# A streaming-encoder block on one core: head transfers, gate merge, last product and row-factor broadcast moved

## The chip, the core and the metric

The kernel runs on one core of a Trainium2 chip. The metric is device microseconds of one execution. The core has TensorE (PE, matmuls; PEld is its weight load), VectorE (DVE), ScalarE (ACT), GpSimd (POOL) and SyncE (SP, which issues most transfers); each works through a queue of its own, in order, and they wait for one another by semaphores.

## The reference, cut to what matters

One layer on x of 256 tokens by 2048 channels, all in float32. Two token mixers (16-head stick-breaking attention and a Mamba-2 state-space scan, "SSD") work on the same normalised input; their outputs are merged by sigmoid gates, projected, normalised and added to x. A gated MLP with a short convolution follows, is normalised and added too.

```python
h = rms_norm(x, norm_mix_pre)                    # row factor * x * gain
proj = h @ w_in
q, k, v, z, xbc, dt, g_sb, g_ssd = split(proj)
o_sb = stick_breaking_attention(q, k, v)
xbc = silu(causal_dwconv(xbc, ssd_conv_w, ssd_conv_b))
dt = softplus(dt + dt_bias)
y = rms_norm((ssd_scan(xs, dt, a, bm, cm) + xs * d_skip) * silu(z), ssd_norm)
merged = sigmoid(g_sb) * (o_sb @ w_sb_proj) + sigmoid(g_ssd) * (y @ w_ssd_proj)
x = x + rms_norm(merged @ w_out, norm_mix_post)
u = causal_dwconv(rms_norm(x, norm_ffn_pre) @ w_up, ffn_conv_w, ffn_conv_b)
gate, val = split(u)
x = x + rms_norm((gelu(gate) * val) @ w_down, norm_ffn_post)
```

## The kernel before

**Weights as a stream.** All weights lie in one array of units of 128 x 1024 floats (512 KB), in the order of use. SP loads each unit into one of five raw buffers (`load`). `prep` splits it: ACT rounds it to a high half (`whi`, L67), DVE subtracts to get the low half (`wlo`, L68); five buffers of each. `unit` hands unit u to the matmuls after it has traced the splits up to u + 3. Activations are split in the same way, and a product is high x high, high x low and low x high, added up in PSUM: two passes with a 512-column and one with a 256-column operand for the "feature" products (`feat_run`, L123 and L125), three 512-column passes for the "token" products (`tok_step`, L152 to L154).

**The order of work.** A compile-time scheduler writes each engine's queue. Among instructions that it reckons ready it takes the one traced first; inside `tc.high_priority()` instructions count as traced at the program's start; inside `tc.manual_schedule(engines=...)` the named engines keep the traced order; `tc.issue_after(ins)` queues what the block traces on `ins`'s engine behind `ins`. From the second SSD group to the end of that stage PE keeps the traced order (L495, closed at L539); before that, and from L541 on, the scheduler orders PE, except in the two hand-written stretches (L726 to L869, and the end from L936).

**The head (L206 to L246).** Twelve wake matmuls on a tile of ones (two passes each) run while the first data come. ACT's queue issues a transfer of the gain `gpre`; SP's queue issues x's first chunk (four k-tiles of x transposed, 512 KB), unit 0 in two halves, unit 1, and then three more chunks of x between units 2 to 4, the vectors and the rest. A hand-written order for ACT and DVE then makes, for each chunk, the high half (ACT, x times gain, L239) and the low half (DVE, L240) of the four k-tiles, with a split of unit 0's first half after two of them and of the second half after four; unit 0's splits are ACT, DVE, ACT, DVE. The first matmuls (`ps_first`, units 0 to 7, `feat_mms`) use them. All products are made with x times gain alone; the row factor of the norm comes in later.

**The row factor of x.** x is loaded once more by rows (`xt`, L249). ACT squares and sums the rows (L482), `rsqrt_mean` makes the factor on DVE and ACT (L280 to L285), all at high priority. `tok_to_bc` (L287) then spreads it: DVE makes two diagonals (`rx_dg`, L293, high priority), PE multiplies ones by them (`rx_ps`, L294), DVE copies the result (`rstd_bc`, L295). It is called after the products `ps_xs` of units 8 and 9 (L503), and once more for the MLP's factor (L898). `dt_work` multiplies by `rstd_bc` (L315), makes softplus in a chain of small DVE and ACT steps, and PE transposes the two results (`dt_pt`, L334 and L335) at a fixed place among the `ps_z` products.

**The merge (L641 to L649).** For each quarter n of the channels, `ps_sb` is finished, DVE multiplies it into the gate (L645) and adds the other mixer's part (L646), for two row tiles; PE then transposes the merged rows (`ptm`, L469) at places among the next products. After n = 3 these are the products `ps_mo`.

**The end (L919 to L955).** The last product `ps_fo` is finished for the first row tile ahead of the second (`tok_mm_lag`). For each row tile, in hand-written order: ACT squares and sums the last 512 columns (`n3.add`, L665), ACT and DVE make a first estimate of the row factor (`n3.last`, L686 to L688), DVE multiplies the PSUM result by the gain (`gained`, L917), DVE refines the factor (`n3.newton`, L692 and L693), and then the rows are scaled, added to x and stored.

Of the kernel before, what the change touches and what calls it, by code (L numbers as in the profile page):

```python
# [10 lines left out]
F32 = mybir.dt.float32  # L11
F32R = mybir.dt.float32r
AF = mybir.ActivationFunctionType
ALU = mybir.AluOpType
# [3 lines left out]
P = 128  # L18
T = 256
KT = 16  # L20
# [7 lines left out]
C_FW = C_CB + 48  # L28
C_FB = C_FW + 88 * 3
C_D = C_FB + 88  # L30
C_N = KT + C_D + 64

LNEXP = "natural_log_exp_and_others"
PE = {mybir.EngineType.PE}
# [5 lines left out]


@with_exitstack
def block_kernel(ctx, tc, xT, xN, wts, vecs, rows, hvec, gain, out):


    nc = tc.nc
    n_units = wts.shape[0]

    const = ctx.enter_context(tc.tile_pool(name="const", bufs=1))
    wraw = ctx.enter_context(tc.tile_pool(name="wraw", bufs=RBUFS))  # L50
    wspl = ctx.enter_context(tc.tile_pool(name="wspl", bufs=WBUFS))
# [7 lines left out]
    def slot(dtype, shape, name):  # L59
        return slots.tile([P] + shape, dtype, tag="slot", name=name)  # L60

    def act_chunk(name):

        return slot(F32R, [4, 2, T], name)

    def split(hi, lo, src):
        nc.scalar.copy(hi, src)  # L67
        nc.vector.tensor_tensor(lo, src, hi.bitcast(F32), op=ALU.subtract)  # L68

    def lnexp():  # L70

        tc.keep_in_program_order(nc.scalar.preload_act_table_set(LNEXP))


    raw_t, spl_t = {}, {}
    state = {"u": 0, "at": 0}

    def load(u, parts=1):
        raw = wraw.tile([P, 1024], F32, tag="raw", name=f"raw{u}")
        n = 1024 // parts  # L80
        for i in range(parts):
            state["load"] = nc.sync.dma_start(raw[:, i * n:(i + 1) * n], wts[u][:, i * n:(i + 1) * n])
        raw_t[u] = raw

    def prep(parts=1):

        v = state["u"]
        state["u"] += 1
        if v not in raw_t:
            load(v)  # L90
        raw = raw_t.pop(v)
        hi = wspl.tile([P, 1024], F32R, tag="whi", name=f"whi{v}")
        lo = wspl.tile([P, 1024], F32R, tag="wlo", name=f"wlo{v}")
        spl_t[v] = (hi, lo)
        n = 1024 // parts
        for i in range(parts):
            w = slice(i * n, (i + 1) * n)
            split(hi[:, w], lo[:, w], raw[:, w])
            yield

    def unit(ahead=WBUFS - 2):
# [31 lines left out]
    def feat_mm(acts, name, ahead=WBUFS - 2):  # L133
        ps = mm_bank(name)
        for u in range(2):
            feat_run(w_tiles(range(8 * u, 8 * u + 8), [ps], ahead), acts, u == 0)
        return ps
# [18 lines left out]
    def tok_mm(acts, nk, name, beats=(3, 7, 11, 15)):  # L156

        pss = [mm_bank(f"{name}_{t}") for t in range(2)]
        for k in range(nk):
            if k % 2 == 0:  # L160
                hi, lo = unit()
            for t in range(2):
                tok_step(pss, acts, k, nk, t, hi, lo)
            for _ in range(beats.count(k % 16)):
                pump()
        return pss
# [34 lines left out]
    def drain():  # L201
        while bg:
            pump()


    ones = const.tile([P, P], F32, name="ones")  # L206
    nc.vector.memset(ones, 1.0)
    wake = paux.tile([P, 512], F32, tag="aux", name="wake")
    for i in range(12):
        nc.tensor.matmul(wake[:, :P], ones, ones, start=True, stop=True)  # L210
    gpre = const.tile([P, KT], F32, name="gpre")
    nc.scalar.dma_start(gpre, vecs[:, 0:KT])
    vec = const.tile([P, C_N - KT], F32, name="vec")
    a_ch, x_raw = [], []
    for c in range(4):
        x_raw.append(slot(F32, [4, T], f"x{c}"))
    raw0 = wraw.tile([P, 1024], F32, tag="raw", name="raw0")
    raw_t[0] = raw0
    nc.sync.dma_start(x_raw[0], xT[:, 0:4, :])
    for i in range(2):  # L220
        nc.sync.dma_start(raw0[:, i * 512:i * 512 + 512], wts[0][:, i * 512:i * 512 + 512])
    load(1)
    for c in range(1, 4):
        nc.sync.dma_start(x_raw[c], xT[:, 4 * c:4 * c + 4, :])
        for u in range(2 * c, min(2 * c + 2, RBUFS)):
            load(u)

    nc.sync.dma_start(vec, vecs[:, KT:])
    hv = const.tile([P, 2], F32, name="hv")
    nc.sync.dma_start(hv, hvec)  # L230
    na = const.tile([P, 1], F32, name="na")
    with tc.manual_schedule(engines=ACT_DVE):
        lnexp()
        for c in range(4):
            ac = act_chunk(f"a{c}")
            steps = prep(2 if c == 0 else 1)
            for j in range(4):
                g = gpre[:, 4 * c + j:4 * c + j + 1]
                nc.scalar.activation(ac[:, j, 0, :], x_raw[c][:, j, :], AF.Copy, scale=g)  # L239
                nc.vector.scalar_tensor_tensor(ac[:, j, 1, :], x_raw[c][:, j, :], g, ac[:, j, 0, :].bitcast(F32), op0=ALU.mult, op1=ALU.subtract)  # L240
                if j == 3 or c == 0 and j == 1:
                    next(steps)
            for _ in prep():
                pass
            a_ch.append(ac)
        nc.scalar.activation(na, hv[:, 1:2], AF.Exp)  # L246
# [40 lines left out]
    def tok_to_bc(dst, src, pool, tag, name):  # L287

        dg = tmp.tile([P, T], F32, tag="diag", name=f"{name}_dg", bufs=1)
        ps = pool.tile([P, 512], F32, tag=tag, name=f"{name}_ps")  # L290
        with tc.high_priority():
            for t in range(2):
                nc.vector.tensor_scalar(dg[:, t * P:(t + 1) * P], ident, src[:, t:t + 1], None, op0=ALU.mult)  # L293
        nc.tensor.matmul(ps[:, :T], ones, dg, start=True, stop=True)  # L294
        nc.vector.tensor_copy(dst, ps[:, :T])  # L295


    cs_dram = dram.tile([64, T], F32, name="cs_dram")
# [194 lines left out]
    for g in range(GROUPS):  # L493
# [3 lines left out]
        for j in range(4):  # L497
# [3 lines left out]
            ps = feat_mm(a_ch, f"ps_xs{g}_{j}")  # L501
# [10 lines left out]
        for j in range(2):  # L512
            ps = feat_mm(a_ch, f"ps_bc{g}_{j}")
# [22 lines left out]
    mrg = [slot(F32, [2048], f"mrg{t}") for t in range(2)]  # L536
# [4 lines left out]
    for n in range(4):  # L541
        ps = tok_mm(y_ch, 32, f"ps_ssd{n}")
        for t in range(2):
            d = mrg[t][:, n * 512:(n + 1) * 512]
# [67 lines left out]
    for hg in range(4):  # L612
        qk = slot(F32, [2, 4, T], f"qk{hg}")
        for i in range(2):
            for h in range(4):
                ps = feat_mm(a_ch, f"ps_qk{hg}_{i}_{h}")
                d = qk[:, i, h, :]
# [18 lines left out]
    def merge_work(n, mc):  # L636
        for t in range(2):
            to_feat(mc, t, gat[t][:, n * 512:(n + 1) * 512], paux, "tp", f"ptm{n}")
            yield

    for n in range(4):  # L641
        ps = tok_mm(o_ch, KT, f"ps_sb{n}")
        for t in range(2):
            d = gat[t][:, n * 512:(n + 1) * 512]
            nc.vector.tensor_tensor(d, d, ps[t], op=ALU.mult)  # L645
            nc.vector.tensor_tensor(d, d, mrg[t][:, n * 512:(n + 1) * 512], op=ALU.add)  # L646
        drain()
        m_ch.append(act_chunk(f"m{n}"))
        bg.append(merge_work(n, m_ch[n]))  # L649
# [55 lines left out]
    for n in range(4):  # L705
        if n < 3:
            ps = tok_mm(m_ch, KT, f"ps_mo{n}")
        else:
            ps, rest = tok_mm_lag(m_ch, KT, f"ps_mo{n}")
# [185 lines left out]
    for j in range(2, FF_T):  # L895
# [8 lines left out]
        if j < 10:  # L904
            t, n = j % 2, (j - 2) // 2
# [10 lines left out]
    def gained(n, t, gfo):  # L916
        nc.vector.tensor_tensor(fo[t][:, blk(n)], ps[t], gfo, op=ALU.mult)  # L917

    for n in range(4):  # L919
        gfo = tmp.tile([P, 512], F32, tag="gfo", name=f"gfo{n}")  # L920
        nc.gpsimd.dma_start(gfo, rows[2, blk(n)].partition_broadcast(P))
        if n < 3:
            ps = tok_mm(f_ch, FF_T, f"ps_fo{n}")
        else:
            ps, rest = tok_mm_lag(f_ch, FF_T, f"ps_fo{n}")
# [10 lines left out]
    with tc.manual_schedule(engines=ACT_DVE | PE):  # L936
        for _ in range(5):
            nc.tensor.matmul(last[:, :P], ones, ones, start=True, stop=True)
        nc.tensor.matmul(last, ident, x2[1][:, blk(0)], start=True, stop=False)
        for t in range(2):  # L940
            n3.add(3, t, ps[t])
            n3.last(t)
            gained(3, t, gfo)
            n3.newton(t)
            r = n3.r[:, t:t + 1]
            if t == 1:
                nc.scalar.activation(r_diag, ident, AF.Copy, scale=r)
                nc.tensor.matmul(last, r_diag, fo[t][:, blk(0)], start=False, stop=True)
                nc.scalar.copy(fo[t][:, blk(0)], last)
                nc.scalar.dma_start(out[t * P:(t + 1) * P, blk(0)], fo[t][:, blk(0)])  # L950
            cuts = [0, 512, 1024, 1536, 2048] if t == 0 else [512, 1024, 1536, 1792, 2048]
            for i, w in enumerate(slice(*c) for c in zip(cuts, cuts[1:])):
                d = fo[t][:, w]
                nc.vector.scalar_tensor_tensor(d, d, r, x2[t][:, w], op0=ALU.mult, op1=ALU.add)
                (nc.scalar if t == 1 and i == 3 else nc.sync).dma_start(out[t * P:(t + 1) * P, w], d)  # L955
# [28 lines left out]
def _cols(v):  # L984

    v = v.reshape(-1, v.shape[-1])
    r, n = v.shape
    return v.reshape(r, n // P, P).transpose(2, 1, 0).reshape(P, n // P * r)
# [48 lines left out]
```

## Time and profile before

| | us |
|---|---|
| median of 3 runs | 2079.42 (2079.32 to 2079.74) |
| the profiled execution | 2079.58 |
| its span, first to last instruction | 2077.9 |
| PE busy | 2070.0 |
| DVE busy | 1382.5 |
| ACT busy | 1162.4 |
| POOL busy | 61.3 |

The granted clock of PE is 0.999 over the span. A row of the timeline reads: start, busy time, engine, line, operation, result<-operands, shapes, count; in brackets the idle time of that engine just before, and what ended it. A "q" behind an engine's name is its sequencer, which issues transfers. A row of the waits reads: who waited, for whom, total us, times, longest. Matmuls are pipelined, so the time from one start to the next says more than the length of one.

### The profile page before, as it was taken

Reading aid. Unit: us, or ns where it says so; the run is one execution under the profiler, and the core shown is the slowest. Engines: PE = TensorE matmul, PEld = TensorE weight load, DVE = VectorE, ACT = ScalarE, POOL = GpSimd, SP = SyncE. Lnnn points to the kernel's source line nnn. Section 1 sums busy time; section 2 is a strip of 40 time slices with the busy share of each in tenths; the row PEclk is TensorE's granted clock in tenths of the full one; section 3 lists DMA queues with packets and bytes.
Section 4 is the critical chain, followed back from the end, with each engine's and each line's share of the span. In section 5 each row is a group of like instructions: output and inputs, shape, how many; then the busy total and the mean of one; then the engine's idle time right before and its main releaser. Section 6 shows DMA issues by size and latency. Waiting matters only on the chain.

```text
span 2077.9 us, 28074 instructions
## 1 busy us (share of the span) xinstructions
PE 2070.0 (100%) x10687; PEld 1772.3 (85%) x10687; DVE 1382.5 (67%) x1868; ACT 1162.4 (56%) x1556; POOL 61.3 (3%) x81
## 2 busy tenths in 40 slices
PE   9999999999999999999999999999999999999998
PEld 8888888888888888888888888888888888888887
DVE  7888887788544445555544576698778778754444
ACT  7767767767543334554656444576556556544443
POOL 0000000000000000000000021000000000000000
PEclk9999999999999999999999999999999999999999
DMA  8666555565555555555555746467565655666653
GB/s 314 215 198 198 189 171 190 187 207 183 179 194 194 194 194 188 167 183 171 173 172 186 271 154 221 141 225 223 192 187 190 191 189 188 192 233 199 198 192 122
DMA packets 109847, 402.81 MB, mean 194 GB/s; under 512 B 12544, under 2 KB 12800, under 8 KB 107664
## 3 DMA queue, kind: packets, MB, share of 16 engines
q1 hardware_dynamic: 106272, 382.72, 56.0%
q0 software_dynamic: 3008, 17.89, 2.6%
q8 instruction: 84, 1.38, 0.3%
q14 instruction: 51, 0.42, 0.1%
q10 hardware_dynamic: 432, 0.40, 0.1%
HBM read 396.71 MB, written 4.26 MB: 193 GB/s over the span
## 4 chain that ended last, share of the span: by engine, by line
PE 96%; DVE 2%; DMA 1%; issue 1%; ACT 0%; SPq 0%; DVEq 0%
PE ps_fv L123 8%; PE ps_fg L123 8%; PE ps_qk L123 6%; PE ps_xs L123 5%; PE ps_fg L125 4%; PE ps_fv L125 4%; PE ps_fo L153 4%; PE ps_fo L152 4%; PE ps_fo L154 4%; PE ps_qk L125 3%; PE ps_ssd L153 3%; PE ps_ssd L152 3%; PE ps_ssd L154 3%; PE ps_z L152 3%; PE ps_z L154 3%; PE ps_z L153 3%
## 5 line engine op out<-in xcount | busy, mean ns | idle before, releaser
L68 DVE TENSOR_TENSOR wlo<-raw,whi 128x1024 fp32r<-128x1024 f32 (+1 forms) x706 | 872.5, 1239 | 481.0 <-ACT whi L67 476.2
L67 ACT CAST whi<-raw 128x1024 fp32r<-128x1024 f32 (+1 forms) x706 | 738.7, 1050 | 547.4 <-PE ps_fo L154 128.7
L123 PE MATMUL ps_fv<-h,whi 128*128 128x512 f32 x688 | 171.6, 391 | 0.0
L123 PE MATMUL ps_fg<-h,whi 128*128 128x512 f32 x688 | 171.1, 391 | 0.0
L123 PEld LDWEIGHTS ps_fv<-h,whi 128*128 128x128 f32 x688 | 126.4, 188 | 24.4
L123 PEld LDWEIGHTS ps_fg<-h,whi 128*128 128x128 f32 x688 | 126.4, 188 | 24.4
L154 PE MATMUL ps_fo<-whi,f 128*128 128x512 f32 x352 | 136.9, 389 | 0.0
L152 PE MATMUL ps_fo<-whi,f 128*128 128x512 f32 x352 | 136.9, 389 | 0.0
L153 PE MATMUL ps_fo<-wlo,f 128*128 128x512 f32 x352 | 136.9, 389 | 0.0
L123 PE MATMUL ps_qk<-a,whi 128*128 128x512 f32 x512 | 125.9, 393 | 0.0
L123 PE MATMUL ps_xs<-a,whi 128*128 128x512 f32 x464 | 116.4, 395 | 0.0
L123 PEld LDWEIGHTS ps_qk<-a,whi 128*128 128x128 f32 x512 | 93.3, 188 | 17.6
L152 PE MATMUL ps_z<-whi,a 128*128 128x512 f32 x256 | 101.5, 396 | 0.0
L154 PE MATMUL ps_z<-whi,a 128*128 128x512 f32 x256 | 99.9, 390 | 0.0
L153 PE MATMUL ps_z<-wlo,a 128*128 128x512 f32 x256 | 99.7, 389 | 0.0
L152 PE MATMUL ps_ssd<-whi,y 128*128 128x512 f32 x256 | 99.6, 389 | 0.0
L153 PE MATMUL ps_ssd<-wlo,y 128*128 128x512 f32 x256 | 99.6, 389 | 0.0
L154 PE MATMUL ps_ssd<-whi,y 128*128 128x512 f32 x256 | 99.6, 389 | 0.0
L123 PEld LDWEIGHTS ps_xs<-a,whi 128*128 128x128 f32 x464 | 84.2, 189 | 16.1 <-issue 0.5
L125 PEld LDWEIGHTS ps_fg<-h,wlo 128*128 128x128 f32 x688 | 88.3, 191 | 3.7 <-DVE wlo L780 0.3
L125 PEld LDWEIGHTS ps_fv<-h,wlo 128*128 128x128 f32 x688 | 88.2, 191 | 3.4
L125 PE MATMUL ps_fg<-h,wlo 128*128 128x256 f32 x688 | 89.5, 283 | 0.0
(301 smaller groups left out, 3543.7 us busy)
## 6 DMA issues: line engine op xcount, KB each, us to landing
raw<-wts SPq DMA_DIRECT2D x713, 512.0 KB, 3.4
csb<-cs_dram POOLq DMA_DIRECT2D x8, 1024.0 KB, 7.1
x<-xT SPq DMA_DIRECT2D x4, 512.0 KB, 7.7
xt<-xN SPq DMA_DIRECT2D x2, 1024.0 KB, 10.9
csb<-gain POOLq DMA_DIRECT2D x8, 256.0 KB, 4.8
xn<-xN POOLq DMA_DIRECT2D x2, 1024.0 KB, 7.9
x_dram<-xn SPq DMA_DIRECT2D x8, 256.0 KB, 5.4
xe<-x_dram POOLq DMA_DIRECT2D x2, 1024.0 KB, 7.9
```

Of the source, the lines that this page charges most:

```text
L67: nc.scalar.copy(hi, src)
L68: nc.vector.tensor_tensor(lo, src, hi.bitcast(F32), op=ALU.subtract)
L123: nc.tensor.matmul(ps, hi, a.rearrange("p s t -> p (s t)"), start=(k == 0), stop=end, skip_group_check=True)
L125: nc.tensor.matmul(ps[:, :T], lo, a[:, 0, :], start=False, stop=end, skip_group_check=True)
L152: nc.tensor.matmul(pss[t], ah, hi[:, w], start=(k == 0), stop=False)
L153: nc.tensor.matmul(pss[t], ah, lo[:, w], start=False, stop=False)
L154: nc.tensor.matmul(pss[t], al, hi[:, w], start=False, stop=(k == nk - 1))
```

## The change

Four edits, and what they need on the host side:

1. *Head.* The gain and x's first two k-tiles are packed into one contiguous array `head` and loaded by one transfer; the other two k-tiles of the first chunk follow unit 0's first half. The other chunks of x are contiguous blocks. The transfer of the gain on ACT's queue goes. Ten wake matmuls instead of twelve. Unit 0 is split as ACT, ACT, DVE, DVE.
2. *Merge.* The low half (DVE) of the first split that is traced after a merge is queued behind the merge's last add.
3. *End.* `gained` stands ahead of `n3.add` and `n3.last`.
4. *Broadcast.* In `tok_to_bc` the matmul and the copy come under high priority too, as the diagonals already did; this holds for both callers.

```diff
-C_N = KT + C_D + 64
+C_N = C_D + 64
...
         for i in range(parts):
             w = slice(i * n, (i + 1) * n)
-            split(hi[:, w], lo[:, w], raw[:, w])
+            with tc.issue_after(state.pop("behind").ins) if "behind" in state else ExitStack():
+                split(hi[:, w], lo[:, w], raw[:, w])
             yield
...
-    for i in range(12):
+    for i in range(10):
         nc.tensor.matmul(wake[:, :P], ones, ones, start=True, stop=True)
-    gpre = const.tile([P, KT], F32, name="gpre")
-    nc.scalar.dma_start(gpre, vecs[:, 0:KT])
-    vec = const.tile([P, C_N - KT], F32, name="vec")
-    a_ch, x_raw = [], []
-    for c in range(4):
-        x_raw.append(slot(F32, [4, T], f"x{c}"))
+    vec = const.tile([P, C_N], F32, name="vec")
+    a_ch = []
+    hd = slot(F32, [KT + 4 * T], "hd")
+    gpre = hd[:, 0:KT]
+    x_raw = [hd[:, KT:].rearrange("p (k t) -> p k t", k=4)] + [slot(F32, [4, T], f"x{c}") for c in range(1, 4)]
...
-    nc.sync.dma_start(x_raw[0], xT[:, 0:4, :])
-    for i in range(2):
-        nc.sync.dma_start(raw0[:, i * 512:i * 512 + 512], wts[0][:, i * 512:i * 512 + 512])
+    n = KT + 2 * T
+    nc.sync.dma_start(hd[:, 0:n], head)
+    nc.sync.dma_start(raw0[:, 0:512], wts[0][:, 0:512])
+    nc.sync.dma_start(hd[:, n:], xT[0:P * 2 * T].rearrange("(p n) -> p n", p=P))
+    nc.sync.dma_start(raw0[:, 512:], wts[0][:, 512:])
     load(1)
     for c in range(1, 4):
-        nc.sync.dma_start(x_raw[c], xT[:, 4 * c:4 * c + 4, :])
+        nc.sync.dma_start(x_raw[c], xT[P * 2 * T:].rearrange("(c p k t) -> c p k t", c=3, p=P, k=4)[c - 1])
...
+    def split_prep():
...
+        at = [slice(0, 512), slice(512, 1024)]
+        nc.scalar.copy(hi[:, at[0]], raw[:, at[0]])
+        yield
+        nc.scalar.copy(hi[:, at[1]], raw[:, at[1]])
+        for w in at:
+            nc.vector.tensor_tensor(lo[:, w], raw[:, w], hi[:, w].bitcast(F32), op=ALU.subtract)
+        yield
...
-            steps = prep(2 if c == 0 else 1)
+            steps = split_prep() if c == 0 else prep()
...
         with tc.high_priority():
             for t in range(2):
                 nc.vector.tensor_scalar(dg[:, t * P:(t + 1) * P], ident, src[:, t:t + 1], None, op0=ALU.mult)
-        nc.tensor.matmul(ps[:, :T], ones, dg, start=True, stop=True)
-        nc.vector.tensor_copy(dst, ps[:, :T])
+            nc.tensor.matmul(ps[:, :T], ones, dg, start=True, stop=True)
+            nc.vector.tensor_copy(dst, ps[:, :T])
...
-            nc.vector.tensor_tensor(d, d, mrg[t][:, n * 512:(n + 1) * 512], op=ALU.add)
+            state["behind"] = nc.vector.tensor_tensor(d, d, mrg[t][:, n * 512:(n + 1) * 512], op=ALU.add)
...
         for t in range(2):
+            gained(3, t, gfo)
             n3.add(3, t, ps[t])
             n3.last(t)
-            gained(3, t, gfo)
             n3.newton(t)
```

More of the change, by code (lines that the diff above doesn't have):

```diff
@@ L42, in block_kernel @@
 @with_exitstack
-def block_kernel(ctx, tc, xT, xN, wts, vecs, rows, hvec, gain, out):
+def block_kernel(ctx, tc, head, xT, xN, wts, vecs, rows, hvec, gain, out):
     nc = tc.nc
@@ L208, in block_kernel @@
     wake = paux.tile([P, 512], F32, tag="aux", name="wake")
-    for i in range(12):
+    for i in range(10):
         nc.tensor.matmul(wake[:, :P], ones, ones, start=True, stop=True)
-    gpre = const.tile([P, KT], F32, name="gpre")
-    nc.scalar.dma_start(gpre, vecs[:, 0:KT])
-    vec = const.tile([P, C_N - KT], F32, name="vec")
-    a_ch, x_raw = [], []
-    for c in range(4):
-        x_raw.append(slot(F32, [4, T], f"x{c}"))
+    vec = const.tile([P, C_N], F32, name="vec")
[3 more added lines that the diff above has]
+    x_raw = [hd[:, KT:].rearrange("p (k t) -> p k t", k=4)] + [slot(F32, [4, T], f"x{c}") for c in range(1, 4)]
     raw0 = wraw.tile([P, 1024], F32, tag="raw", name="raw0")
     raw_t[0] = raw0
-    nc.sync.dma_start(x_raw[0], xT[:, 0:4, :])
-    for i in range(2):
-        nc.sync.dma_start(raw0[:, i * 512:i * 512 + 512], wts[0][:, i * 512:i * 512 + 512])
+    n = KT + 2 * T
[3 more added lines that the diff above has]
+    nc.sync.dma_start(raw0[:, 512:], wts[0][:, 512:])
     load(1)
     for c in range(1, 4):
-        nc.sync.dma_start(x_raw[c], xT[:, 4 * c:4 * c + 4, :])
+        nc.sync.dma_start(x_raw[c], xT[P * 2 * T:].rearrange("(c p k t) -> c p k t", c=3, p=P, k=4)[c - 1])
         for u in range(2 * c, min(2 * c + 2, RBUFS)):
             load(u)
-    nc.sync.dma_start(vec, vecs[:, KT:])
+    nc.sync.dma_start(vec, vecs)
     hv = const.tile([P, 2], F32, name="hv")
@@ L231, in block_kernel @@
     na = const.tile([P, 1], F32, name="na")
+    def split_prep():
+        state["u"] += 1
+        hi = wspl.tile([P, 1024], F32R, tag="whi", name="whi0")
+        lo = wspl.tile([P, 1024], F32R, tag="wlo", name="wlo0")
+        spl_t[0] = (hi, lo)
+        raw = raw_t.pop(0)
+        at = [slice(0, 512), slice(512, 1024)]
[5 more added lines that the diff above has]
+        yield
     with tc.manual_schedule(engines=ACT_DVE):
@@ L1016 @@
     wts = np.concatenate([t.reshape(-1, P, 1024) for t in parts], axis=0)
-    vecs = np.concatenate([_cols(arr(t)) for t in (norm_mix_pre, ssd_conv_w, ssd_conv_b, ffn_conv_w, ffn_conv_b)]
+    xT = x.T.reshape(KT, P, T).transpose(1, 0, 2)
+    flat = lambda a: a.reshape(-1)
+    vecs = np.concatenate([_cols(arr(t)) for t in (ssd_conv_w, ssd_conv_b, ffn_conv_w, ffn_conv_b)]
                           + [np.broadcast_to(arr(d_skip), (P, 64))], axis=1)
     arrays = {
-        "xT": x.T.reshape(KT, P, T).transpose(1, 0, 2),
+        "head": np.concatenate([_cols(arr(norm_mix_pre)), xT[:, 0], xT[:, 1]], axis=1),
+        "xT": np.concatenate([flat(xT[:, 2:4])] + [flat(xT[:, 4 * c:4 * c + 4]) for c in range(1, 4)]),
         "xN": x,
```

## The prediction

> **What bounds the kernel now.** I read the page first, then the waits of TensorE, then the timeline around each place that the diff touches. On the page:
>
> ```profile
> span 2077.9 us, 28074 instructions
> PE 2070.0 (100%) x10687; PEld 1772.3 (85%) x10687; DVE 1382.5 (67%) x1868; ACT 1162.4 (56%) x1556; POOL 61.3 (3%) x81
> PE 96%; DVE 2%; DMA 1%; issue 1%; ACT 0%; SPq 0%; DVEq 0%
> ```
>
> TensorE (PE) is busy all but 7.9 us of the span, and the chain that ended last is 96% PE. No part of the diff adds or removes a matmul of the computation (two wake matmuls go), so only three things can move the time: when PE starts on real work, the stalls inside its stream, and the tail after its last matmul. The profiled execution took 2079.58 us, span 2077.9 plus 1.7 around it; the median of the three runs shown, 2079.42, is 0.16 below it, so I make the sum in differences and add it to the median. The four places follow, each with its rows.
>
> **The head.** Rows of the timeline, then of the view of DMA issues for the first 2.1 us (last column: us to landing), then of the windows (PE busy, clock, DMA share, GB/s):
>
> ```profile
> 1.12 5.49 PE L210 MATMUL wake<-ones 128*128 128x128 f32 x24 [1.12 <-DVE ones L207]
> ...
> 2.17 0.43 SPq L82 DMA_DIRECT2D raw<-wts  x1
> ...
> 5.05 0.91 ACT L239 ACTIVATE a<-x,gpre 128x256 fp32r<-128x256 f32 x2 [2.52 <-DMA gpre<-vecs]
> ...
> 5.86 0.60 ACT L67 CAST whi<-raw 128x512 fp32r<-128x512 f32 x1
> ...
> 6.51 0.75 PE L123 MATMUL ps_first<-a,whi 128*128 128x512 f32 x2
> ...
> 7.64 1.83 PE L123 MATMUL ps_first<-a,whi 128*128 128x512 f32 x6 [0.37 <-DVE a L240]
> ...
> 11.28 2.00 ACT L67 CAST whi<-raw 128x1024 fp32r<-128x1024 f32 x2
> ...
> 13.04 2.00 PE L123 MATMUL ps_first<-a,whi 128*128 128x512 f32 x8
> ```
> ```profile
> x<-xT SPq DMA_DIRECT2D x1, 512.0 KB, 4.0
> gpre<-vecs ACTq DMA_DIRECT2D x1, 8.0 KB, 4.2
> ```
> ```profile
> 2.00:4.00 2.00, 2.00 (x11) 1.00 0.78 248
> ```
>
> ACT's first product waits for the gains, issued at 0.80 and landed 4.2 later, at about 5.0; x lands 0.2 before that. Two products (0.91) and half a split (0.60) lead to PE's first matmul at 6.51, and the stream becomes dense at 7.64, when the low halves of x's next k-tiles are there. After the change one transfer of 264 KB brings what 520 KB brought; 256 KB less at 248 GB/s is 1.0 us. So the first product starts near 4.0, the first matmul near 5.5, and the dense stream near 6.6: the DVE now makes those low halves ahead of the weight's. The twelve wake matmuls (24 passes, 0.229 us each) end at 6.6; ten end at 5.7, so they do not stand in the way. SyncE issues one transfer more ahead of the later loads, 0.43 us, while those loads queue behind data anyway; ScalarE's queue loses one. Not all of 1.0 us lasts: the third weight unit's high half is made by 12.28 (half of the 2.00) and used at 13.04, a slack of 0.76, and it waits on transfers whose bytes ahead are unchanged. I take 0.75 us gained, bounds 0 and 1.05.
>
> **The row factor's broadcast.** Rows of the timeline from 27.8 to 39.3:
>
> ```profile
> 27.79 1.92 ACT L482 ACTIVATE xt<-xt 128x2048 f32<-128x2048 f32 x1 [0.49 <-DMA xt<-xN]
> ...
> 29.80 2.00 PE L123 MATMUL ps_xs<-a,whi 128*128 128x512 f32 x8
> 29.83 0.17 DVE L280 TENSOR_SCALAR rx_v<-ss_x 128x2 f32<-128x2 f32 x1 [4.23 <-ACT xt L482]
> ...
> 32.73 1.05 ACT L67 CAST whi<-raw 128x1024 fp32r<-128x1024 f32 x1
> ...
> 33.68 0.38 ACT L146 COPY cvr<-ps_first 128x256 f32<-128x256 f32 x1
> ...
> 33.94 0.48 DVE L293 TENSOR_SCALAR rx_dg<-ident,rstd_tok 128x128 f32<-128x128 f32 x2
> ...
> 34.46 0.75 DVE L147 TENSOR_TENSOR cvr<-cvr,ps_first 128x256 f32<-128x256 f32 x2
> ...
> 35.13 1.22 DVE L68 TENSOR_TENSOR wlo<-raw,whi 128x1024 fp32r<-128x1024 f32 x1
> ...
> 35.40 0.60 PE L294 MATMUL rx_ps<-rx_dg,ones 128*128 128x256 f32 x2
> ...
> 38.87 0.42 DVE L295 COPY rstd_bc<-rx_ps 128x256 f32<-128x256 f32 x1
> ```
>
> Here the change moves a matmul (L294, two passes) and its copy (L295). The copy gains: it now stands behind three weight splits and one sum and ends at 39.3 though its input was done at 36.0; raised, it goes ahead of most of them. The matmul is the danger. Engines take their queue in order, and the queue was written by a scheduler that puts a raised instruction where it reckons its input ready. In this chain that reckoning is early by about four microseconds, and the rows show it: rx_v, raised already, held the DVE idle 4.23 us, because the squares of x's rows (L482) waited for their transfer. Had it not, the diagonal (L293) would have been done not at 34.42 but at 30.2, when PE is one or two matmuls into ps_xs, which start at 29.80. A second sign gives the same place: in the DVE's queue the second sum of L147 stands ahead of the split at 35.13, though the split's input (ACT, 32.73) was made before the sum's (ACT, 33.68). A scheduler that takes what is ready picks so only if the diagonal kept the DVE until the second-last result of ps_first was copied; so in its reckoning the diagonal ended as ps_first ends, just ahead of 29.80.
>
> At normal priority the matmul came behind all of ps_xs, at 35.40, and waited for nothing. Raised, it goes into the queue near 30.2. PE comes there at 29.45 (0.75 earlier) and waits until 34.45: the transfer of x's rows sets that, its queue is full of the same bytes, and the weights behind the matmul cannot pass it. That is 5.0 us idle; against before it is 34.45 − 30.2 = 4.25 us lost, the head's gain already spent in it. Bounds: 0, if it stays behind 34.45, and 4.9, if it goes a few matmuls ahead of 29.80. ACT and DVE run only into full weight buffers meanwhile. The second caller of the helper (r2, L898) finds the same raise, but there PE's matmul already stands between matmuls of a later group, as early as its input allows, so I cost it at nothing; if it moved ahead of its input it would cost tenths.
>
> **The clock after the wait.** Rows of the windows at the end of the run (PE busy, granted clock, DMA share, GB/s), and of the timeline:
>
> ```profile
> 2072.00:2074.00 2.00, 0.79 (x2) 1.00 0.61 217
> 2074.00:2076.00 2.00, 0.00 (x0) 0.76 0.96 303
> 2076.00:2077.90 1.90, 0.00 (x0) 0.50 0.02 6
> ```
> ```profile
> 2069.18 1.28 PE L938 MATMUL last<-ones 128*128 128x128 f32 x10
> ```
>
> PE's last matmul ends at 2072.79. A mean of 0.76 over the next-but-one window is full clock until 2075.04 and half after it: 2.25 us without matmuls bring the half clock. The same 128-column passes take 0.128 us in L938 and 0.229 in the wake matmuls, all 24 of them, 5.5 us long. So a wait of 5.0 us should be followed by about 5 us at half clock, half of which is lost: 2.5 us, bounds 0 and 3.4.
>
> The Trainium skill, in TensorE: Matmul & The Clock Gate (Part 1, the HAM clock gate), says that an idle window of about 3.4 us halves the clock, that one busy window of that length restores it, and that the windows run free of the kernel. By that rule alone the loss would be at least 1.7 us, and a wait under 3.4 us might cost no clock; the trace agrees in kind, and its drop 2.25 us after the last matmul is earlier than a whole idle window.
>
> **The dt transposes.** Timeline:
>
> ```profile
> 56.28 0.39 PE L154 MATMUL ps_z<-whi,a 128*128 128x512 f32 x1
> ...
> 57.31 0.33 PE L335 MATMUL dt_pt<-ident,dts 128*128 128x128 f32 x1 [0.20 <-DVE dts L329]
> 57.39 0.48 PE L152 MATMUL ps_z<-whi,a 128*128 128x512 f32 x1
> ```
>
> From 56.28 to 57.39 PE does one 512-column pass and two transposes. The passes of ps_xs come every 0.23 us (eight in 2.00, the last one's 0.39 included) and two short ones take 0.26 by L938, so 0.62 is stall, on the chain that begins with the copy at 38.87. With the copy some 3 us earlier the stall goes in either case: −0.6 us. Next late is nothing before the merge.
>
> **The merge.** Timeline:
>
> ```profile
> 1246.03 3.48 DVE L68 TENSOR_TENSOR wlo<-raw,whi 128x1024 fp32r<-128x1024 f32 x3
> ...
> 1249.43 1.27 DVE L645 TENSOR_TENSOR gat<-gat,ps_sb 128x512 f32<-128x512 f32 x2
> ...
> 1250.68 0.39 PE L154 MATMUL ps_mo<-whi,m 128*128 128x512 f32 x1
> 1251.45 0.63 PE L469 MATMUL ptm<-ident,gat 128*128 128x128 f32 x4 [0.39 <-DVE gat L646]
> ```
>
> PE passes from 1250.68 to 1251.45, 0.77 where 0.23 is due: 0.54 lost to the gate merge behind three splits of 1.16 each. The change queues one of them behind the merge, so L646 ends 1.16 earlier and the stall goes: −0.54. The split that now waits is used three units later, and its raw buffer comes free that much later: hidden, at nothing; uncovered it would cost up to 1.16 at one place.
>
> **The tail.** Timeline:
>
> ```profile
> 2070.17 0.69 DVE L917 TENSOR_TENSOR fo<-ps_fo,gfo 128x512 f32<-128x512 f32 x1
> ...
> 2070.42 0.20 ACT L687 ACTIVATE n_r<-n_q 128x1 f32<-128x1 f32 x1
> ...
> 2070.77 0.21 DVE L692 SCALAR_TENSOR_TENSOR n_q<-n_r,n_m 128x1 f32<-128x1 f32 x1
> ```
>
> ACT's estimate is done at 2070.62, the DVE's product ends at 2070.86 and Newton's first step starts at 2070.77. With the product moved ahead into the time of the squares, the step starts at about 2070.67: −0.1, bounds 0 and −0.15.
>
> **Sum.** +4.25 + 2.5 − 0.6 − 0.54 − 0.1 = +5.5 on 2079.42: **2084.9 us**, the head's 0.75 lost in the wait.
>
> **Rivals.** (1) *The wait, but the clock holds.* The drop at the end of the run is one sighting; against this stands that 5.0 us is over twice 2.25. +3.0: 2082.4 us. (2) *No wait*, and the kernel is faster: the matmul lands in the queue behind the point where PE passes 34.45. For it: the head is reordered too, which can move the scheduler's reckoning, and a few matmuls' shift of the reckoning shortens the wait microsecond for microsecond; it decides from about 18 matmuls later. Then −0.75 − 0.6 − 0.54 − 0.1 = −2.0: 2077.4 us. Against: two signs put it at 30.2. (3) *The raise changes nothing* (the matmul stays at its boundary) and the copy alone moves: the same 2077.4; without the copy's gain 2078.0.
>
> **How the numbers follow.** 0.2%, 4.2 us, is about what a measurement of this kernel can tell from no change. Forecast 0.42 (its own range 2083.0 to 2086.8, the bounds of wait and clock), rival 1 0.20, rivals 2 and 3 0.33, anything else, such as a worse head, 0.05. Slower by over 0.2% is above 2083.6: most of the forecast, 0.37, and 0.03 of the rest: 0.40. Faster than 2075.3 has no case: 0.02. The rest, 0.58, is within 0.2%, though the likeliest single case is not. Range 2077.0 to 2086.5.
>
> **What would show it.** Right: two rx_ps passes among the first matmuls of ps_xs with an idle of some 5 us put down to the DVE's rx_dg, granted clock near 0.5 for the next 3 to 7 us, first real matmul near 5.5, no wait on dt_pt and ptm, L692 0.1 sooner after the last ps_fo. Wrong: rx_ps without a wait, or at the boundary to ps_bc; then rival 2 or 3 holds. If rx_ps waits and the 128x512 passes behind it stay at 0.23 us, rival 1.

## The result, and the profile after

| | before | after |
|---|---|---|
| median, us | 2079.58 | 2086.81 (2086.06 to 2087.57, 6 runs) |
| the profiled execution, us | 2079.58 | 2086.79 |
| its span, us | 2077.9 | 2085.1 |

The changed kernel takes 1.0034 times as long, 95% interval 1.0025 to 1.0044: 7.2 us more, where 5.5 were forecast. Single executions far off the rest (2564.7 of the kernel before here, 6888.7 in run 7 below) are left out of the ratios, though not of the medians.

The page of the kernel after, the rows that answer to the first fence of the prediction, and then its waits of TensorE:

```profile
span 2085.1 us, 28061 instructions
PE 2071.1 (99%) x10683; PEld 1773.7 (85%) x10683; DVE 1383.8 (66%) x1868; ACT 1164.6 (56%) x1556; POOL 61.4 (3%) x81
```
```profile
PE rx_ps L312 <- DVE rx_dg L311: 4.9, 1, 4.9
PE last L966 <- ACT r_diag L965: 2.0, 1, 2.0
PE wake L211 <- DVE ones L208: 1.1, 1, 1.1
PE ps_first L124 <- DVE a L258: 0.5, 1, 0.5
```

PE is 14.0 us short of the span where it was 7.9. Two waits are new in size: 4.9 us at the raised matmul, which was forecast, and 2.0 us at the very end, which was 0.35 before and was not forecast. The waits at the transposes `dt_pt` and `ptm` are gone from the list.

The timeline of the head and of the broadcast, after:

```profile
3.54 0.91 ACT L257 ACTIVATE a<-hd 128x256 fp32r<-128x256 f32 x2 [1.46 <-DMA hd<-head]
...
5.41 0.78 PE L124 MATMUL ps_first<-a,whi 128*128 128x512 f32 x2
...
6.72 1.13 PE L124 MATMUL ps_first<-a,whi 128*128 128x512 f32 x3 [0.53 <-DVE a L258]
...
29.06 0.39 PE L124 MATMUL ps_xs<-a,whi 128*128 128x512 f32 x1
...
33.81 0.48 DVE L311 TENSOR_SCALAR rx_dg<-ident,rstd_tok 128x128 f32<-128x128 f32 x2
...
34.35 1.22 PE L312 MATMUL rx_ps<-rx_dg,ones 128*128 128x256 f32 x2 [4.90 <-DVE rx_dg L311]
...
35.01 3.55 PE L124 MATMUL ps_xs<-a,whi 128*128 128x512 f32 x7
...
36.13 0.42 DVE L313 COPY rstd_bc<-rx_ps 128x256 f32<-128x256 f32 x1
```

The first real matmul starts 1.10 earlier and `ps_xs` 0.74 earlier. Behind one matmul of `ps_xs` PE stands still until the diagonal is there; the seven passes that follow take 3.55 us, where the eight of before took 2.00. The windows of the same stretch (PE busy, PEld, DVE, ACT and POOL busy, granted clock, DMA share, GB/s) say why:

```profile
29.40:34.30 4.90, 0.05 (x1) 0.00 (x0) 3.77 (x10) 4.83 (x12) 0.00 (x0) 0.85 0.83 300
34.40:39.60 5.20, 5.20 (x15) 4.34 (x16) 5.05 (x11) 1.76 (x4) 0.00 (x0) 0.50 0.69 222
38.00:40.00 2.00, 2.00 (x11) 1.90 (x10) 1.61 (x5) 1.38 (x3) 0.00 (x0) 0.57 0.61 209
40.00:42.00 2.00, 2.00 (x14) 1.80 (x13) 1.89 (x6) 1.18 (x3) 0.00 (x0) 1.00 0.60 234
```

A mean of 0.85 over 4.90 us is 3.4 us at full and 1.5 us at half clock: it fell at about 32.85, 3.4 us into the wait, and stayed at half through the dense matmuls behind it. The window 38 to 40, with a mean of 0.57, puts its return at about 39.7.

The transposes of dt and of the merge, after:

```profile
63.12 0.39 PE L155 MATMUL ps_z<-whi,a 128*128 128x512 f32 x1
63.36 0.27 PE L352 MATMUL dt_pt<-ident,dts 128*128 128x128 f32 x1
63.47 0.27 PE L353 MATMUL dt_pt<-ident,dts 128*128 128x128 f32 x1
63.49 0.48 PE L153 MATMUL ps_z<-whi,a 128*128 128x512 f32 x1
```
```profile
1256.74 0.39 PE L155 MATMUL ps_mo<-whi,m 128*128 128x512 f32 x1
1256.97 0.60 PE L487 MATMUL ptm<-ident,gat 128*128 128x128 f32 x4
```

From the pass before the transposes of dt to the one behind them PE takes 0.37 us (before 1.11), from the last `ps_mo` to `ptm` 0.23 (before 0.77). Both stalls are gone. The second caller's matmul (`r_ps`, L312) still stands between two matmuls of `ps_fv` and waits for nothing.

The end. First rows of the kernel before that the prediction did not show, then those of after:

```profile
2066.09 0.68 DVE L917 TENSOR_TENSOR fo<-ps_fo,gfo 128x512 f32<-128x512 f32 x1
...
2067.13 2.74 DVE L954 SCALAR_TENSOR_TENSOR fo<-fo,n_r,xe 128x512 f32<-128x512 f32 x4
...
2068.94 0.40 PE L154 MATMUL ps_fo<-whi,f 128*128 128x512 f32 x1
...
2069.38 0.60 ACT L665 ACTIVATE n_j<-ps_fo 128x512 f32<-128x512 f32 x1 [2.84 <-PE ps_fo L154]
...
2071.21 0.40 ACT L947 ACTIVATE r_diag<-ident,n_r 128x128 f32<-128x128 f32 x1 [0.59 <-DVE n_r L693]
```
```profile
2071.57 0.60 ACT L683 ACTIVATE n_j<-ps_fo 128x512 f32<-128x512 f32 x1 [9.19 <-DVE fo L935]
...
2073.30 2.74 DVE L972 SCALAR_TENSOR_TENSOR fo<-fo,n_r,xe 128x512 f32<-128x512 f32 x4
...
2074.49 0.39 PE L155 MATMUL ps_fo<-whi,f 128*128 128x512 f32 x1
...
2075.96 0.68 DVE L935 TENSOR_TENSOR fo<-ps_fo,gfo 128x512 f32<-128x512 f32 x1
2076.68 0.60 ACT L683 ACTIVATE n_j<-ps_fo 128x512 f32<-128x512 f32 x1 [3.86 <-DVE fo L935]
...
2078.41 0.40 ACT L965 ACTIVATE r_diag<-ident,n_r 128x128 f32<-128x128 f32 x1 [0.48 <-DVE n_r L711]
```

Before, ACT squares the second row tile's last columns as soon as `ps_fo` is finished (2068.94 + 0.40 = 2069.34, squares at 2069.38), while the DVE is still busy with the first tile's four sums (until 2069.87). After, `ps_fo` is finished at 2074.88, and the squares start 1.80 later, released by the DVE's product: that product stands in the DVE's queue behind the first tile's sums (until 2076.04) and ahead of the squares. Where the extra time arises, by the starts of the same products in the two timelines:

| start of | before | after | difference |
|---|---|---|---|
| `ps_xs` | 29.80 | 29.06 | −0.74 |
| `ps_bc` | 35.65 | 42.70 | +7.05 |
| `ps_z` | 46.98 | 53.83 | +6.85 |
| `ps_qk` | 773.93 | 780.01 | +6.08 |
| `ps_fg` | 1350.33 | 1355.79 | +5.46 |
| last `ps_fo` | 2068.94 | 2074.49 | +5.55 |
| `r_diag` | 2071.21 | 2078.41 | +7.20 |

### The profile page after: what moved, and what is told of

Its sections match the earlier page's. It is cut to its first block, busy times and chain, and to the rows that moved or that the text cites. A ratio compares the mean times of both kernels' runs of the same rounds, so it can differ in the third digit from the quotient of the medians.

```text
span 2085.1 us, 28061 instructions
## 1 busy us (share of the span) xinstructions
PE 2071.1 (99%) x10683; PEld 1773.7 (85%) x10683; DVE 1383.8 (66%) x1868; ACT 1164.6 (56%) x1556; POOL 61.4 (3%) x81
## 4 chain that ended last, share of the span: by engine, by line
PE 97%; DMA 1%; DVE 1%; ACT 0%; issue 0%; SPq 0%; DVEq 0%; ACTq 0%
PE ps_fv L124 7%; PE ps_fg L124 7%; PE ps_qk L124 6%; PE ps_xs L124 5%; PE ps_fv L126 4%; PE ps_fg L126 4%; PE ps_fo L154 4%; PE ps_fo L153 4%; PE ps_fo L155 4%; PE ps_qk L126 3%; PE ps_bc L124 3%; PE ps_z L155 3%; PE ps_z L153 3%; PE ps_z L154 3%; PE ps_ssd L153 3%; PE ps_ssd L155 3%
## 5 line engine op out<-in xcount | busy, mean ns | idle before, releaser
L68 DVE TENSOR_TENSOR wlo<-raw,whi 128x1024 fp32r<-128x1024 f32 x704 | 870.7, 1240 | 476.8 <-ACT whi L67 472.1
L67 ACT CAST whi<-raw 128x1024 fp32r<-128x1024 f32 x704 | 737.6, 1051 | 559.3 <-PE ps_fo L155 128.7
```

## The experiments

The theory: the raised matmul makes PE wait and halves its clock, the head's gain is spent in that wait, and the end costs 1.65 because two readers of one PSUM result are ordered, so that the squares wait for the product and the product for the first tile's sums. The rivals: the extra time at the end is only the shift of everything before it; the wait is hidden or harmless and the loss comes from elsewhere.

**1. The old end.** The changed kernel with `gained` back in its place; the same edit, reversed, on the kernel before is run 2.

```diff
-            gained(3, t, gfo)
             n3.add(3, t, ps[t])
             n3.last(t)
+            gained(3, t, gfo)
             n3.newton(t)
```

> The changed kernel with the old order at the end (squares, estimate, product, refinement). Theory: at the end the product of the second row tile had to wait for the DVE's four sums of the first tile, and the squares on ACT then waited for the product, 1.65 us in all; 2086.8 - 1.65 = 2085.1 us, and the end from the last ps_fo matmul to r_diag is 1.9 us again. Rival: the squares were late for another reason (stores of the first tile, the clock), so the old order brings at most 0.2: 2086.6 us.

2085.34 (2084.12 to 2086.66), ratio 1.0028 (1.0017 to 1.0039): 1.5 below the changed kernel, as the theory had it; in its timeline `r_diag` starts 2.27 us after the last `ps_fo` does, as in the kernel before (3.92 in the changed kernel). The profiled execution (2086.66) is the slowest of its series: PE waits 6.2 us at the raised matmul in it, since the diagonal is there only at 36.2.

**2. The new end alone**, in the kernel before.

> The kernel before with the product ahead of the squares at the end and nothing else. Theory: 2079.5 + 1.65 = 2081.1 us, squares of the second tile waiting for the product. Prediction's step: 2079.5 - 0.1 = 2079.4 us.

2081.19 (2080.70 to 2081.99) against 2079.53: +1.66. The interval of the ratio, 0.9997 to 1.0016, takes in no change, but all 10 runs lie above 23 of the 24 of before, and the timeline shows the mechanism without the rest of the change:

```profile
2067.43 2.74 DVE L954 SCALAR_TENSOR_TENSOR fo<-fo,n_r,xe 128x512 f32<-128x512 f32 x4
...
2070.08 0.68 DVE L917 TENSOR_TENSOR fo<-ps_fo,gfo 128x512 f32<-128x512 f32 x1
2070.80 0.60 ACT L665 ACTIVATE n_j<-ps_fo 128x512 f32<-128x512 f32 x1 [3.85 <-DVE fo L917]
```

**3. The squares first, then the product.** The changed kernel with the squares put back to the front, so that of the end's new order only the product ahead of the estimate is left; the matmul of the broadcast is at normal priority, its copy raised (as in run 7).

```diff
+            n3.add(3, t, ps[t])
             gained(3, t, gfo)
-            n3.add(3, t, ps[t])
             n3.last(t)
             n3.newton(t)
```

> The changed kernel with the broadcast's matmul at normal priority, and with the end in the order squares, product, estimate, refinement. Theory: two engines do not read the same PSUM result at once here, the program orders them: the product starts only when the squares of the second tile have been read out, the estimate's DVE step comes behind it, and the refinement starts about 0.2 us later than in the old order: 2079.7 us. Rival: the product runs beside the squares as soon as the DVE is free, and the refinement starts 0.1 us sooner: 2079.4 us. The start of the product against the end of the squares decides, not the time.

A single time, 2078.94. What it tells is the order, in its timeline:

```profile
2069.02 0.19 ACT L684 ACTIVATION_READ_ACCUMULATOR n_j<-ps_fo 128x1 f32 x1
...
2069.25 0.69 DVE L936 TENSOR_TENSOR fo<-ps_fo,gfo 128x512 f32<-128x512 f32 x1
...
2070.11 0.22 DVE L711 SCALAR_TENSOR_TENSOR n_q<-n_r,n_m 128x1 f32<-128x1 f32 x1
```

The DVE is free and the result is there, but the product starts only when the squares are read out (2069.21): the later reader waits for the earlier one, whichever comes first in the program. That is the readers' order shown from the other side. Here it makes `r_diag` 0.2 later against the last `ps_fo` than in the old order, no gain.

**4. The raise alone**, in the kernel before.

```diff
-        nc.tensor.matmul(ps[:, :T], ones, dg, start=True, stop=True)
-        nc.vector.tensor_copy(dst, ps[:, :T])
+            nc.tensor.matmul(ps[:, :T], ones, dg, start=True, stop=True)
+            nc.vector.tensor_copy(dst, ps[:, :T])
```

> The kernel before with the broadcast's matmul and copy raised and nothing else. Theory: the matmul stands at the head of ps_xs, PE waits there from 29.8 to 34.4 us (4.6), runs at half clock for some 5 us after it (2.5 lost), and the dt transposes no longer wait (-0.7): 2079.5 + 6.4 = 2085.9 us. Rival: the wait comes from the new head, which lets PE run ahead of its data; then 2079.5 - 0.7 = 2078.8 us.

2085.91 (2085.00 to 2086.13), ratio 1.0030 (1.0018 to 1.0041): +6.4. The row of its waits:

```profile
PE rx_ps L294 <- DVE rx_dg L293: 4.6, 1, 4.6
```

So the wait needs no other edit; the reordered head does not cause it.

**5. The wait filled with work.** The changed kernel, with 22 matmuls of ones on ones queued between the first matmul of `ps_xs` and the raised one. They compute nothing that is used. (`state["pe"]` is the matmul that `feat_run` queued last.)

```diff
+                if k == 0 and high:
+                    state["first"] = state["pe"]
...
-            nc.tensor.matmul(ps[:, :T], ones, dg, start=True, stop=True)
+            if name == "rx":
+                with tc.issue_after(state["first"].ins):
+                    for _ in range(22):
+                        f = nc.tensor.matmul(ps[:, T:T + P], ones, ones, start=True, stop=True)
+            with tc.issue_after(f.ins) if name == "rx" else ExitStack():
+                nc.tensor.matmul(ps[:, :T], ones, dg, start=True, stop=True)
```

> The changed kernel with 22 more matmuls of ones by ones, into an unused part of rx_ps's bank, queued on PE between the first matmul of ps_xs and the broadcast's matmul. Theory: the data set the wait, so the broadcast still runs at about 34.4 us; but PE is busy meanwhile (22 x 0.22 = 4.8 us), the clock stays full and the 2.7 us behind the wait are not lost: 2086.8 - 2.7 = 2084.1 us, 128x512 matmuls behind rx_ps 0.23 us apart. Rival: those matmuls are slow because the weights or the DVE are late after the wait; then 2086.8 us or more, and they stay 0.43 us apart.

2084.34 (2083.83 to 2086.36), ratio 1.0023 (1.0014 to 1.0033): 2.5 below the changed kernel, although PE gets to the rest no earlier. Its timeline and its window behind the raised matmul:

```profile
29.11 5.07 PE L319 MATMUL rx_ps<-ones 128*128 128x128 f32 x44
34.36 0.70 PE L321 MATMUL rx_ps<-rx_dg,ones 128*128 128x256 f32 x2 [0.18 <-DVE rx_dg L315]
34.71 1.98 PE L124 MATMUL ps_xs<-a,whi 128*128 128x512 f32 x7
```
```profile
34.40:36.40 2.00, 2.00 (x9) 1.69 (x10) 2.00 (x4) 0.76 (x2) 0.00 (x0) 1.00 0.85 274
```

The clock holds, and the same seven passes take 1.98 us instead of 3.55. This parts the two costs that came together: the wait, and the clock behind it, 2.5 us by the medians.

**6. Half the wait.** The changed kernel, with the raised matmul queued behind unit 8's last matmul (`state["half"]`), in the middle of `ps_xs`.

```diff
+            if u == 0:
+                state["half"] = state["pe"]
...
-            nc.tensor.matmul(ps[:, :T], ones, dg, start=True, stop=True)
+            with tc.issue_after(state["half"].ins) if name == "rx" else ExitStack():
+                nc.tensor.matmul(ps[:, :T], ones, dg, start=True, stop=True)
```

> The changed kernel with the broadcast's matmul queued behind unit 8's last matmul instead of ps_xs's first. Theory: PE comes 2.8 us of work later to the same wait, some 2.4 us are left of it, and the whole difference is won: 2086.8 - 2.7 = 2084.1 us if the clock falls all the same (at the end of the run 2.25 us without matmuls brought the half clock), and 2081.4 us if so short a wait leaves the clock alone; runs may fall on either side. Rival, the wait does not shorten (it follows the place in the queue and not the data): 2086.8 us.

2082.91 (2081.21 to 2084.10), ratio 1.0015 (1.0006 to 1.0025), in two groups: four runs from 2081.2 to 2081.9 and six from 2082.8 to 2084.1. The profiled run (2083.51) belongs to the second; its windows:

```profile
33.00:35.40 2.40, 0.84 (x5) 0.79 (x6) 2.32 (x10) 2.40 (x5) 0.00 (x0) 1.00 0.89 265
35.60:38.80 3.20, 3.20 (x12) 2.71 (x11) 3.20 (x5) 0.71 (x1) 0.00 (x0) 0.50 0.72 250
39.00:41.00 2.00, 2.00 (x10) 1.66 (x9) 1.96 (x7) 0.65 (x2) 0.00 (x0) 1.00 0.87 252
```

A wait of 2.45 us halved the clock for 3.4 us in this run, at a time when PE was already busy again. That the first group are runs in which the clock held fits the 1.7 us that this costs, but only one run was profiled, and the mean clocks on record, 0.998 or 0.999 in both groups, do not tell them apart.

**7. The matmul at normal priority, the copy raised, the old end.** What the prediction's third rival prices.

```diff
-            nc.tensor.matmul(ps[:, :T], ones, dg, start=True, stop=True)
+        nc.tensor.matmul(ps[:, :T], ones, dg, start=True, stop=True)
+        with tc.high_priority():
             nc.vector.tensor_copy(dst, ps[:, :T])
```

> The changed kernel with the old order at the end, and with the broadcast's matmul at normal priority (its copy stays raised). Theory: the matmul goes back behind ps_xs, the wait of 4.9 us and the half clock behind it (2.7 us) go. But the copy, raised alone, stands in the DVE's queue where it stood before, so the dt transposes, reached 0.74 us sooner, wait 0.74 us longer and eat the head's gain; the merge's 0.6 is left: 2079.5 - 0.6 = 2078.9 us. Rival (the prediction's): the raised copy alone frees the dt transposes: 2077.4 us.

2079.46 (from 2078.50), ratio 1.0003 (0.9993 to 1.0013): no change that could be told. The rival's 2077.4 (0.9990) lies outside the interval; the theory's 2078.9 (0.9997) lies inside, so the time does not part it from no change. By the rows, `ps_xs` starts 0.62 earlier than in the kernel before, the transposes of dt 0.31 later, `ps_fg` 0.34 earlier again: the head's gain is gone at the transposes, and about 0.6 comes from the merge. In its timeline the copy stands where it stood, behind the same two splits of weights, and the transposes of dt wait as before:

```profile
36.90 2.35 DVE L68 TENSOR_TENSOR wlo<-raw,whi 128x1024 fp32r<-128x1024 f32 x2
39.17 0.41 DVE L314 COPY rstd_bc<-rx_ps 128x256 f32<-128x256 f32 x1
```
```profile
PE dt_pt L353 <- DVE dts L347: 0.3, 1, 0.3
PE ps_xs L126 <- DVE wlo L68: 0.2, 1, 0.2
PE dt_pt L354 <- DVE dts L348: 0.2, 1, 0.2
```

Raising the copy moves nothing as long as the matmul that it reads from is not raised too.

**8. The head alone.** The changed kernel with the broadcast, the merge and the end as before.

> The changed kernel with merge, end and broadcast as before: the head alone. Theory: PE gets to ps_xs 0.74 us sooner, but the dt transposes wait for a chain that begins with x's rows, whose transfer is no earlier, so they wait 0.74 us longer: 2079.5 us. Rival: the head's gain reaches the end: 2078.8 us.

2079.66 (2079.24 to 2080.16), ratio 1.0000 (0.9990 to 1.0009): no gain that could be told, though the interval holds the rival's 2078.8 (0.9997) too. In the profiled run (2079.24, span 2077.5) the first matmul is 1.4 earlier, at 5.13, but the stream is dense only at 7.16:

```profile
7.16 1.82 PE L124 MATMUL ps_first<-a,whi 128*128 128x512 f32 x6 [1.29 <-DVE a L258]
```

So `ps_xs` starts 0.48 earlier than in the kernel before, and 0.33 of that is left at the transposes of dt and still at the last `ps_fo`. The theory had all of it lost at the transposes.

**9 and 10. The transposes of dt later on PE.** If what holds PE up there is work on the other engines, other PE work in front of it should cover it. Head and merge of the change, broadcast and end as before; the two runs move the places, among the 16 k-tiles of `ps_z`, at which PE takes up the next step of the first SSD group: the first three of five by one or two places, or the first alone by one. (Run 10's expectation speaks of all four beats moved in run 9; it was three.)

```diff
-BEATS0 = (6, 10, 12, 14, 15)
+BEATS0 = (8, 11, 13, 14, 15)     # run 9
+BEATS0 = (7, 10, 12, 14, 15)     # run 10
```

> The changed kernel's head and merge, with the old end and the broadcast at its old priority, and the dt transposes moved two k-tiles later among the ps_z products (beats 8, 11, 13, 14, 15 instead of 6, 10, 12, 14, 15). Theory: PE has 2.7 us more work ahead of the transposes, so they wait for nothing, and the head's 0.74, the transposes' 0.7 and the merge's 0.6 all reach the end: 2079.5 - 2.0 = 2077.5 us. Rival: what follows the transposes (sums, decays, the first group) becomes late in its turn and gives the 1.4 us back: 2078.9 us.

2078.47 (2078.03 to 2082.61), ratio 0.9995 (0.9986 to 1.0004).

> The change's contiguous head and its early merge, the broadcast and the end as in the kernel before, and only the first of the four beats that follow x's transposes moved by one unit, so that the transposes of dt stand one unit later on TensorE. Theory: what holds TensorE up at them (0.30 + 0.39 us in the kernel before, 0.44 + 0.39 with the contiguous head) is work of the other engines that a unit of 1.36 us in front of them covers, and the beats behind keep their distance, so that no wait of 1.1 us arises at the cumulative sums as in the run with all four beats moved: 0.5 to 0.8 for the transposes and 0.3 to 0.6 for the merge, so about 2078.0 to 2078.5 against 2079.4. Rival: the same beat moved late by one unit only hands the wait on to the sums behind it, 2079.0 to 2079.5.

2078.62 (2077.67 to 2080.51) against 2079.51, ratio 0.9996 (0.9987 to 1.0005). Both medians are 0.9 below the kernel before, and neither interval excludes no change, though 8 and 7 of their 11 runs lie below the lowest of before. In run 10 the transposes of dt wait no more, and the wait is handed on to the sums `pd`, as its rival had it, but a small one:

```profile
84.93 1.97 PE L465 MATMUL pd<-xw,mm 128*128 128x64 f32 x16 [0.29 <-DVE mm L433]
```

By the timelines of runs 8 and 10, which differ in this beat and in the merge, run 10 is 0.55 ahead before `pd` and 0.1 behind it. What is left of its gain by these timelines is mostly the merge's 0.54. Run 9's profiled execution is the slowest of its series; PE waits 1.1 there for the same operand, and its windows show what a short wait can do:

```profile
85.20:86.20 1.00, 0.00 (x0) 0.00 (x0) 1.00 (x2) 1.00 (x2) 0.05 (x1) 1.00 0.64 148
86.20:87.80 1.60, 1.53 (x14) 1.56 (x15) 1.56 (x3) 1.25 (x3) 0.00 (x0) 1.00 0.91 110
88.00:91.30 3.30, 3.30 (x11) 2.62 (x10) 3.21 (x8) 3.00 (x5) 0.00 (x0) 0.50 0.96 370
```

One microsecond idle and sixteen 64-column matmuls, and the clock is at half for the next 3.3 us. So no version was shown to beat the kernel before; the nearest is 0.9 us below it, 0.04%.

## Why the prediction was wrong in its size

**The step that failed is the tail.** It put "−0.1, bounds 0 and −0.15", "with the product moved ahead into the time of the squares". Measured: +1.65 between the last `ps_fo` and `r_diag`. The step asked neither what the moved product waits for nor who waits for it. First, and this the rows of before show, the time of the squares (2069.38 to 2069.98) was not free on the DVE: the first row tile's sums run until 2069.87, over nearly all of it. Second, and this they do not show, because there the product stands behind the estimate anyway, squares and product read the same PSUM result, and the program orders two such readers; so the product, put ahead, holds the squares back. The price from the rows: the squares start 1.80 instead of 0.04 after the last `ps_fo`, +1.76, of which 0.63 is the first tile's own end, later by the same order (its sums end 1.16 instead of 0.53 after the last `ps_fo`), and the rest the product's 0.68 and the part of the sums that the squares used to overlap. From the squares to `r_diag` it is 1.73 instead of 1.83: the 0.1 that was forecast is there, and it is the small part. Runs 1 and 2 show the sum from both sides (−1.5 and +1.66), run 3 the order of readers.

The Trainium skill, in PSUM — Partial Sum Buffer (PSUM bank collisions raise a hardware error), says that two engines may not access the same bank and quadrant at once, two reads included, and that the compiler back end therefore puts a dependency between them. The traces agree: in the end's rows of before, after and run 3, ACT and DVE never read one `ps_fo` at the same time (in after the product ends at 2076.64 and the squares start at 2076.68). With that rule asked for, "moved ahead into the time of the squares" could not have been written.

**The broadcast's wait: right.** Forecast near 30.2 in PE's queue and 5.0 us idle until 34.45; it is one matmul behind 29.06 and idle until 34.35, 4.9 in the waits' row. Run 4 shows that the raise alone does it. The signs in the DVE's queue led to the right place. The length is the transfer's: in run 1's profiled execution, where the last squares of x's rows (L500) could start only at 29.54 instead of 27.67, the same wait is 6.2. The second caller costs nothing, as forecast.

**The clock: right in kind, its size in part by luck.** 2.5 forecast. Half clock under running matmuls from 34.35 to about 39.70 makes 2.7; run 5 gives 2.5. The bounds, 0 and 3.4, held it. But the forecast took the time at half clock from the length of the wait, and the traces do not bear that out: the half clock ends on a grid (below) that lies differently in each execution. In run 1's profiled execution the wait is longer, 6.2, and the half clock behind it shorter, from 36.22 to 40.80, which makes 2.3.

**The head: right for the change, too much by itself.** `ps_xs` starts 0.74 earlier (0.75 forecast) and the wait spends it. But rival 2's and 3's sums counted it as a gain that lasts to the end; run 8's time shows none, and its rows 0.33.

**The dt transposes: right in the change, wrong in the third rival.** The stall goes with the raise (0.74 by the rows, 0.6 forecast). The copy then ends at 36.55 instead of 39.3, but PE also comes to the transposes 6.6 later, which alone would cover the stall; no run parts the two. In run 7, where only the copy is raised, it keeps its place and the stall stays; there the rival's 2077.4 was 2 us too low, 0.75 + 0.6 of it by head and dt.

**The merge: right.** 0.54 by the rows, as forecast. Runs 4 and 8, without this edit, keep a wait of 0.4 at `ptm`. The split that waits instead shows in no wait of PE.

Up to the last `ps_fo` the steps sum to 4.25 + 2.5 − 0.6 − 0.54 = +5.6, and +5.55 was measured. That it fits so closely is in part luck: by the table it is 7.05 against 6.75 at `ps_bc` and −1.50 against −1.14 behind it. The error of the whole, 7.2 against 5.5, is the tail's 1.75. The forecast's "own range 2083.0 to 2086.8, the bounds of wait and clock" is not what its bounds add up to: at the upper ones, 4.9 and 3.4, the sum is 2086.5.

## What to carry to other kernels

Before an instruction is moved ahead on an in-order engine, look up in the trace what that engine does at the new time and who else reads the same PSUM result: where the program orders such readers, as here, a reader put ahead of another engine's delays it by its whole wait and length, even if both only read. A raise in priority is a raise in the scheduler's reckoning, and where the trace shows that reckoning early (an engine idle before a raised instruction), a raised matmul can make the whole matmul stream wait. An idle stretch on PE can cost more than its length: price the half clock behind it, and try filler matmuls where the stretch can't be removed.

## What the runs showed of the hardware

The clock's changes lie on a grid. In the trace of after it fell at 32.88 and came back at 39.70, 6.83 us apart, twice 3.41; in run 6 it was at half from 35.49 to 38.90 and in run 9 from 87.95 to 91.37, once 3.41 each. The clock's records in all twelve traces agree: every stretch between two changes is a whole number of 3.413 us (in after 27.31 at full, 6.83 at half and 2041.17 at full: 8, 2 and 598). The first rise comes between 4.08 and 7.05 us after the first instruction, so the grid does not start with the kernel. In runs 6 and 9 PE worked through the whole stretch at half clock, and that did not shorten it. In the changed kernel the clock stayed at half for two such stretches: in the first, PE worked only from 34.35 on, and the second followed.

A stretch need not be idle from end to end for the clock to fall: 2.45 us of waiting were enough in run 6, and in run 9 about 1.1 us and sixteen 64-column passes. Cut the traces into these windows of 3.413 us, and the timelines show how much work was enough, as far as the modelled ends of the matmuls can tell. At full clock, windows in which PE was busy for up to 0.43 of the time were followed by half clock (run 4, 2077.36 to 2080.77), and those with 0.49 or more were not (run 2, 2069.32 to 2072.74), but for the one of run 9, 0.68 and mostly 64-column passes. At half clock, up to 0.74 (run 7, 0.22 to 3.64) did not bring the full clock back, and 0.87 or more did (run 8, 0.66 to 4.08). By an estimate from these shares a window may be idle for 1.7 to 1.9 us, so a wait of 2.45 us is harmless where an edge of the grid parts it near its middle, in about a third of the executions; in run 6 the first group is four of ten.

The Trainium skill, in TensorE: Matmul & The Clock Gate (Part 1, the HAM clock gate), has the fall after an idle window of about 3.4 us, in windows that run free of the kernel. The length and the free grid agree with these runs, which would also explain run 6's two groups; an idle window, read as one without any matmul, does not. No run varied the busy share on purpose.
